# Two hybrid layers on one core: score products of the keys' low parts over all 128 rows, in key blocks of 512 and 256 columns

## The chip, the cores and the metric

The kernel runs on one core of a Trainium2 chip. The metric is the device time of one execution in microseconds (us). Before the change the median of three runs is 2503.3 us (2502.24 to 2503.67).

## The reference, cut to what matters

Two layers act on 512 latent tokens and 256 context tokens with 2048 features. A layer modulates its input, projects it, passes three groups of columns on (a short convolution, differential attention, pooling), gates them, projects back and normalizes. The change lies in the attention. There are 8 heads; each has two halves of 64 features, and for each half a score of a query block against all keys:

```python
s = jnp.einsum('bqhid,bkhid->bhiqk', qb * ATTN_SCALE, k_all)   # i: the two halves, d: 64 features
p = jax.nn.softmax(s, axis=-1)
a = p[:, :, 0] - lam * p[:, :, 1]
return jnp.einsum('bhqk,bkhe->bqhe', a, v_all)
```

Latent queries see 768 keys (context and latents). In the first layer the context's queries see the 256 context keys; in the second layer the context has no queries. All arrays are float32, and the kernel keeps nearly that precision.

## The kernel before, in words

**Precision by parts.** Each float32 operand x is split into a high part (a copy in the type F32R, made by ScalarE) and a low part (x minus the high part, made by VectorE). A product of two operands is then three matmuls, high x high, high x low, low x high, that add up in one PSUM bank (mm3, line 322).

**Weights.** WStream (line 144) loads pieces of 128x512 floats through SyncE's queue into six rotating buffers raw (RAW = 6, line 146). `_split` (line 164) copies one to wh on ScalarE, subtracts on VectorE into wl, and issues the load that follows; four pairs wh and wl rotate (BUFS = 4). Until late in the startup two raw loads stand ahead; from then on as many as there are buffers (line 440).

**Order.** The program is written out by hand. Every engine works through its own instructions in order; a matmul "slot" of the projections ends with pump() (line 220), which runs the due steps (later, line 217), one step of the attention of a head (att), and, if VectorE's estimated time leaves room, one step of the background queue (modq), which computes modulation vectors on VectorE from weights that are loaded by SyncE (mod_gen, line 462). The estimates are dve_cost and pe_cost (lines 65 and 72).

**Stages.** In each layer: four feature tiles and v (startup for layer 0, line 370; lines 1220 to 1241 for layer 1), the remaining feature tiles with the attention of the heads beside them (mtile, line 738, called in line 1259), then the output projection (gemm2, line 1066). TensorE's work of the feature tiles is interleaved with that of the attention.

**Head tiles.** alloc_head_tiles (line 520) makes for each layer the tiles Q (tag z2, 2048 columns), K (three rows of 768), aT and v (2048 columns). Q and v have unused tails of 512 columns, and the background work writes its unneeded elementwise results there (Z["jk"], lines 524 and 530). v_evac (line 535) uses the first 1024 columns of Q, v, K and aT for evacuating the rows of v.

**Queries and keys of a head.** For the halves i = 0 and 1, Q[:, i] has 128 rows: the 64 high parts and the 64 low parts of that half. The high parts stand in rows 0 to 63 for i = 0 and in rows 64 to 127 for i = 1. K[:, i] has the high parts of the keys of that half twice, in both groups of rows, so that one full-row product gives high x high and low x high. The low parts of the keys are in K[:, 2]: half 0 in rows 0 to 63, half 1 in rows 64 to 127 (ev_k, line 812; los, lines 825 and 826). So the product with the low parts uses 64 rows only (hi, line 599). rq is the work row of 768 columns in which queries and keys are turned.

**A score** (score, line 597) has a step mm, which issues the products (lines 615 to 618), and a step ex, which takes the maximum on VectorE (line 623) and the exponential on ScalarE (line 624), both from PSUM. For 768 keys, four products are issued: full-row for keys 0 to 383 and 384 to 767, in a bank each, then 64-row for the same; for the 256 context keys one of each. Two PSUM pairs SS are used in turn by the scores and the transposes of the result (trans, line 640); pvmm (line 666) then multiplies by v. A layer 0 head has 4 query blocks with 768 keys and 2 with 256, a layer 1 head 4 with 768, each for two halves.

Of the kernel before, what the change touches and what calls it, by code (L numbers as in the profile page):

```python
# [10 lines left out]
F32 = mybir.dt.float32  # L11
# [30 lines left out]
class Timed:  # L42
    """an engine, with an estimate of the time that its queue takes"""

# [33 lines left out]
def body(tc, A, out):  # L78
# [4 lines left out]
    with tc.tile_pool(name="sb", bufs=1) as sb, tc.tile_pool(  # L83
# [3 lines left out]
        def st(shape, name, dt=F32, tag=None, bufs=1):  # L87
            return sb.tile(shape, dt, name=name, tag=tag or name, bufs=bufs)

# [1 line left out]
        ident = st([P, P], "ident")  # L91
# [22 lines left out]
        edge = st([P, 4, 16], "edge")  # L114
        pw = st([P, P], "pw")
        neglam = st([P, 2], "neglam")
        sc1 = st([P, KT, 2], "sc1")
# [19 lines left out]

# [1 line left out]
        wseq = []  # L139
# [4 lines left out]
        class WStream:  # L144
            """weights: DRAM -> raw -> exact high and low parts"""
            BUFS, RAW = 4, 6

# [48 lines left out]

# [1 line left out]
        att = deque()  # L198
# [21 lines left out]
        def pump(n=1):  # L220
            for _ in range(n):
                slotn[0] += 1
                for fn in due.pop(slotn[0], ()):
                    fn()
                step(att)
                # the background takes what time VectorE has left
                V.t = max(V.t, PE.t - LAG)
                credit[0] = min(credit[0] + rate[0], 3.0)
                if modq and credit[0] >= 1 and V.t < PE.t - left[0]:
                    credit[0] -= 1  # L230
                    step(modq)
# [6 lines left out]

# [1 line left out]
        S.dma_start(out=bm, in_=A["bm"])  # L240
# [11 lines left out]
        def silu2_into(dst, tmp):  # L252
            """dst = 2 * silu(dst)"""
            S.activation(out=tmp, in_=dst, func=AF.Tanh, scale=0.5)
            V.scalar_tensor_tensor(out=dst, in0=tmp, scalar=1.0, in1=dst, op0=ALU.add, op1=ALU.mult)
# [14 lines left out]

        # consumption order of the projections' weights
        first4 = [M_CC, M_CU, M_CB, M_CG]
# [16 lines left out]
        lt = [layer_tiles(l) for l in range(2)]  # L289
        # pieces of the last weights that wait on chip: split beside these pairs  # L290
        SIDE = [(1, 3), (1, 6)] + [(2, j) for j in range(8)]
# [18 lines left out]

        # token accumulators of the token-major products
        accs = [lat[0], lat[1], SS[0][:, 0], SS[0][:, 1], SS[1][:, 0], SS[1][:, 1]]

        # what can be read after the products of a token, as a pair of banks is waited for as a whole
        ready = [[0], [1], [], [2, 3], [], [4, 5]]
# [16 lines left out]

# [1 line left out]
        # The scales come first: the feature tiles are of the scaled rows and get the shifts' part as a bias  # L334
        # later, the rows of v are of the whole h.
        NB = 4
# [33 lines left out]
        def startup():  # L370
# [11 lines left out]
            silu2_into(srows[0], pp.rearrange("p a b -> p (a b)")[:, 0:JD])  # L382
            # the other row to all partitions
            for j in range(0, JD, 512):
# [75 lines left out]

# [1 line left out]
        def mod_gen(tiles, nv, kcs, buf, rows=None):  # L462
            """acc: from the modulation's weights, or bv: the shifts' part of the first tiles"""
            sbm, rawm, jk = buf
# [35 lines left out]
        class Cvt:  # L500
            """rotating use of the three wide scratch rows"""

# [15 lines left out]
        Z = {}  # L518

        def alloc_head_tiles(l):  # L520
            q = st([P, 2048], f"Q_{l}", F32R, tag="z2")
            Z["Q"] = q[:, 0:2 * T].rearrange("p (a b) -> p a b", a=2)
            Z["Qf"] = q
            Z["jk"] = q[:, 2 * T:2 * T + KCH]
            Z["K"] = st([P, 3, T], f"K_{l}", F32R, tag="z0")
            Z["a"] = st([P, 2, 6, 256], f"aT_{l}", F32R, tag="z1")
            v = st([P, 2048], f"v_{l}", F32R, tag="z3")
            Z["v"] = v[:, 0:12 * P].rearrange("p (a b c) -> p a b c", a=2, b=6)
            Z["vf"] = v
            Z["jk"] = (Z["jk"], v[:, 12 * P:12 * P + KCH])  # L530

# [30 lines left out]

# [1 line left out]
        lb = [0]  # L564
# [19 lines left out]
        def attention(l, h):  # L584
# [12 lines left out]
            def score(t, qt, i):  # L597
                box = {}
                hi = slice(0, 64) if i == 0 else slice(64, 128)
                qs = slice(qt * P, qt * P + P)  # L600
# [4 lines left out]
                def mm():  # L605
                    s = box["t"] = next_S()
                    if qt < 4:
                        box["s"] = s[:, :, 0:384]
                        parts = [(s[:, 0, 0:384], 0), (s[:, 1, 0:384], 384)]
                        n = 384  # L610
                    else:
                        box["s"] = s[:, 0, 0:256]
                        parts = [(box["s"], 512)]
                        n = 256
                    for ap, k0 in parts:
                        PE.matmul(ap, lhsT=Q[:, i, qs], rhs=K[:, i, k0:k0 + n], start=True, stop=False)
                    for ap, k0 in parts:
                        PE.matmul(ap, lhsT=Q[hi, i, qs], rhs=K[hi, 2, k0:k0 + n], start=False, stop=True)
                    scores_left[0] -= 1

                def ex():
                    sv = box["s"]
                    V.tensor_reduce(out=sm[:, i:i + 1], in_=sv, axis=AX.XY if qt < 4 else AX.X, op=ALU.max, negate=True)
                    S.activation(out=po.rearrange("p (a b) -> p a b", a=2) if qt < 4 else po, in_=sv, func=AF.Exp,  # L624
                                 bias=sm[:, i:i + 1], scale=1.0, accum_out=sm[:, 2 + i:3 + i])
                    free_S(box["t"])
# [39 lines left out]
            def pvmm(t, u):  # L666
# [5 lines left out]
                def mm():  # L672
                    # beside the closed half of the features' bank that is not in use
                    pv = box["p"] = cps[(lb[0] + 1) % 2][:, 256:512]
                    for j, kt in enumerate(kts):
                        mm3(pv, v[:, 0, kt], v[:, 1, kt], a[:, 0, kt], a[:, 1, kt], j == 0, j == n - 1)
# [9 lines left out]
            scores_left[0] = 2 * nq  # L686
            # distances of the steps, in steps: two of them to a slot in layer 0, one in layer 1
            t, gs, gt, gp, dx, dn, dc, dl, dv, ge, gf = PAR[l]
# [46 lines left out]

# [1 line left out]

# [34 lines left out]
        def silu2(tmp, pl, pc, ctx):  # L772
            """tmp = 2 * silu(psum)"""
            for ps, a, b in segs(pl, pc, ctx):
# [4 lines left out]
        def rope():  # L779
# [7 lines left out]
            cvt.give(i)  # L787

        lo_, hi_ = slice(0, 64), slice(64, 128)

# [21 lines left out]
        def ev_k(l, h, pl, pc):  # L812
# [11 lines left out]
            def los():  # L824
                V.tensor_sub(out=K[lo_, 2], in0=rq[lo_], in1=K[lo_, 0].bitcast(F32))
                V.tensor_sub(out=K[hi_, 2], in0=rq[hi_], in1=K[hi_, 1].bitcast(F32))

# [148 lines left out]

# [1 line left out]
        yrow = lambda s: cv[:, s % 3, 0:T] if s % 6 < 3 else pp[:, s % 3, :]  # L978
# [14 lines left out]

# [1 line left out]
        def gate_row(t0, i, j):  # L995
# [8 lines left out]
        def h_affine():  # L1004
            for i in range(2):
                # h = n * (g (1 + sc)) + (b (1 + sc) + sh)
                V.tensor_scalar(out=hA[:, :, i], in0=acc[:, 32:48, i], scalar1=1.0, scalar2=None, op0=ALU.add)
# [58 lines left out]
        def gemm2(l):  # L1066
# [85 lines left out]
            flush()  # L1152
            # the last part token by token, so that the norms follow closely
            S.activation(out=rst[:, 0:1], in_=epsc, func=AF.Sqrt)
# [19 lines left out]
            else:  # L1174
# [5 lines left out]
                for t in range(4):  # L1180
# [4 lines left out]
                    S.activation(out=r, in_=mv[:, t, 1:2], func=AF.Sqrt, bias=epsc, scale=1.0)  # L1185
                    # a part of the first rows goes another way, so that VectorE keeps up with the products
                    own = hv[:1] if t < 2 else hv
# [16 lines left out]

# [1 line left out]
        for l in range(2):  # L1206
# [12 lines left out]
            else:  # L1219
                # four feature tiles of the latents, as their h arrives  # L1220
                for k in range(KT):
# [117 lines left out]
```

## Time and profile before

| what | value |
|---|---|
| median of three runs | 2503.3 us (2502.24 to 2503.67) |
| span of the profiled execution, first to last instruction | 2499.2 us |
| the profiled execution's own time | not listed apart; the median is 4.1 us over its span |
| TensorE (PE) busy | 2462.3 us, 99% |
| TensorE weight loads (PEld) busy | 2032.7 us, 81% |
| VectorE (DVE) busy | 1696.4 us, 68% |
| ScalarE (ACT) busy | 927.8 us, 37% |
| GpSimd (POOL) busy | 121.0 us, 5% |
| moved by DMA | 353.64 MB, 141 GB/s |
| mean granted TensorE clock, as a share of the full one | 0.995 |

The profile comes from one execution. Busy time is the union of an engine's instructions. Matmuls are pipelined and overlap, so a matmul's listed duration is longer than what it costs in a dense stream; the distance between the starts of neighbours is the cost. Every matmul has a weight load of its own, listed under PEld, which can run beside the matmul ahead of it. In square brackets a row tells how long the engine was idle before it, and which instruction's end released it.

### The profile page before, as it was taken

What the parts mean: (1) busy time and instruction counts of PE and PEld (TensorE: products, weight loads), DVE (VectorE), ACT (ScalarE), POOL (GpSimd) and SP (SyncE); (2) the same over time, 40 slices, a digit from 0 to 9 for tenths busy, and PEclk for the clock granted to TensorE, in tenths of its full rate; (3) what the DMA queues carried; (4) which work ended last, traced back from release to release, by engine and by line L of the source; (5) the groups of instructions that cost most, each with busy time, mean ns of one, the idle gap of its engine ahead of it and who ended that gap; (6) DMA issues with size and microseconds to landing.
All of it is one profiled execution on the core that took longest, in us unless ns stands there. A gap on an engine that the chain in (4) does not pass through costs nothing. (4 is left out here: it accounts for less than half of the span.)

```text
span 2499.2 us, 33724 instructions
## 1 busy us (share of the span) xinstructions
PE 2462.3 (99%) x12501; PEld 2032.7 (81%) x12501; DVE 1696.4 (68%) x3252; ACT 927.8 (37%) x1668; POOL 121.0 (5%) x197
## 2 busy tenths in 40 slices
PE   8999999999999999999999999999999999999997
PEld 7887888888888888888888778888878887887885
DVE  8894868677677778755486663256676666666656
ACT  4551434333343434433211253134444434444321
POOL 0000000000000000001100000000000000000202
PEclk9999999999999999999999999999999999999998
DMA  9886634343443434334455532253443434423653
GB/s 337 311 294 201 203 107 115 104 114 106 117 115 95 125 103 123 91 91 137 168 172 172 178 114 89 97 184 93 120 127 111 118 98 128 122 81 110 201 157 131
DMA packets 182168, 353.64 MB, mean 141 GB/s; under 512 B 19217, under 2 KB 43937, under 8 KB 181234
## 3 DMA queue, kind: packets, MB, share of 16 engines
q1 hardware_dynamic: 144946, 293.88, 37.0%
q0 software_dynamic: 36912, 57.55, 8.2%
q8 instruction: 98, 1.61, 0.3%
q14 instruction: 68, 0.56, 0.1%
q10 hardware_dynamic: 144, 0.05, 0.0%
HBM read 319.89 MB, written 31.51 MB: 141 GB/s over the span
## 5 line engine op out<-in xcount | busy, mean ns | idle before, releaser
L53 DVE TENSOR_TENSOR wl<-raw,wh 128x512 fp32r<-128x512 f32 x566 | 384.4, 689 | 384.9 <-ACT wh L173 383.5
L53 PE MATMUL lat<-hhl,wh 128*128 128x512 f32 x1472 | 603.7, 410 | 1.6 <-DVE Q L53 1.6
L173 ACT CAST wh<-raw 128x512 fp32r<-128x512 f32 x566 | 346.5, 618 | 663.4 <-PE SS L53 289.5
L53 PE MATMUL lat<-hll,wh 128*128 128x512 f32 x1472 | 583.5, 396 | 0.0
L53 PE MATMUL lat<-hhl,wl 128*128 128x512 f32 x1472 | 582.8, 396 | 0.0
L53 PEld LDWEIGHTS lat<-hhl,wh 128*128 128x128 f32 x1472 | 277.8, 189 | 71.8 <-issue 22.0
L53 PEld LDWEIGHTS lat<-hhl,wl 128*128 128x128 f32 x1472 | 277.8, 189 | 65.1
L53 PE MATMUL cps<-hc,wh 128*128 128x256 f32 x1664 | 318.9, 285 | 0.1
L53 PEld LDWEIGHTS lat<-hll,wh 128*128 128x128 f32 x1472 | 278.3, 189 | 43.2 <-DVE hll L53 0.3
L53 PEld LDWEIGHTS cps<-hc,wh 128*128 128x128 f32 x1664 | 275.2, 189 | 39.5 <-issue 8.5
L624 ACT ACTIVATE pp<-SS,smt 128x768 f32<-128x768 f32 (+1 forms) x160 | 130.7, 817 | 355.1 <-DVE smt L53 349.6
L53 PE MATMUL cps<-hc,wl 128*128 128x256 f32 x832 | 231.5, 278 | 0.0
L53 PE MATMUL SS<-wh,hc 128*128 128x512 f32 x512 | 171.1, 393 | 0.4 <-DVE aT L53 0.3
L53 PEld LDWEIGHTS cps<-hc,wl 128*128 128x128 f32 x832 | 156.4, 188 | 0.0
L53 PE MATMUL SS<-K,Q 128*128 128x384 f32 (+1 forms) x576 | 155.6, 361 | 0.7 <-DVE aT L53 0.7
L53 PE MATMUL lat<-wl,hhl 128*128 128x512 f32 x364 | 144.9, 398 | 6.8 <-DVE wl L53 6.8
L53 PE MATMUL lat<-wh,hhl 128*128 128x512 f32 x364 | 146.3, 402 | 0.5 <-DVE o L53 0.5
L53 DVE TENSOR_REDUCE smt<-SS 128x1 f32<-128x768 f32 (+1 forms) x160 | 135.4, 846 | 16.7 <-PE SS L53 16.7
L53 PE MATMUL lat<-wh,hll 128*128 128x512 f32 x364 | 143.1, 393 | 0.0
L53 PEld LDWEIGHTS SS<-K,Q 128*128 128x128 f32 (+1 forms) x576 | 94.9, 186 | 48.0 <-issue 35.0
L53 DVE CUSTOM_DVE_ANT_0 pp<-cv,acc 128x512 bf16<-128x512 f32 x112 | 80.0, 748 | 52.2 <-DMA cv<-in_wmbg_dram 37.8
L53 PEld LDWEIGHTS SS<-wh,hc 128*128 128x128 f32 x512 | 96.3, 188 | 22.9 <-DVE aT L53 1.2
(263 smaller groups left out, 3561.9 us busy)
## 6 DMA issues: line engine op xcount, KB each, us to landing
raw<-in_wa_dram SPq DMA_DIRECT2D x352, 256.0 KB, 2.7
m<-in_wmbg_dram SPq DMA_DIRECT2D x200, 256.0 KB, 2.7
raw<-in_wo_dram SPq DMA_DIRECT2D x128, 256.0 KB, 3.2
wb<-in_wm0b_dram SPq DMA_DIRECT2D x32, 704.0 KB, 7.1
raw<-in_wv_dram SPq DMA_DIRECT2D x64, 256.0 KB, 3.3
cv<-in_wmbg_dram SPq DMA_DIRECT2D x56, 256.0 KB, 2.7
cv<-in_xT_dram SPq DMA_DIRECT2D x32, 384.0 KB, 4.9
v<-vsc POOLq DMA_DIRECT2D x32, 384.0 KB, 6.0
```

The source lines that it names most:

```text
L53: return fn(*a, **k)
L173: S.copy(out=h, in_=r)
L624: S.activation(out=po.rearrange("p (a b) -> p a b", a=2) if qt < 4 else po, in_=sv, func=AF.Exp, bias=sm[:, i:i + 1], scale=1.0, accum_out ...
```

## The change

The keys' low parts get rows of zeros, so that they have 128 rows. For half 0 they remain in K[:, 2], whose rows 64 to 127 are now zero. For half 1 they move to the tail of Q (512 columns) and the last 256 columns of v, with zeros in rows 0 to 63. The zeros are written once per layer: GpSimd fills rq with zeros, and ScalarE copies from it. The low products use the whole of Q[:, i]; key blocks are now 512 and 256 columns, and the order is high, low for each block. The subtraction for half 1 becomes two. The unneeded results of the background work go to a tile jk of their own in bfloat16, and the raw buffers are five. Scores of 768 keys are read from PSUM as one flat row. Comment lines that the diff only empties are left out here.

```diff
@@ persistent tiles
+        jk = st([P, KCH], "jk", BF16)
@@ class WStream
-            BUFS, RAW = 4, 6
+            BUFS, RAW = 4, 5
@@ alloc_head_tiles
+        lo_, hi_ = slice(0, 64), slice(64, 128)
+
         def alloc_head_tiles(l):
             q = st([P, 2048], f"Q_{l}", F32R, tag="z2")
...
-            Z["jk"] = q[:, 2 * T:2 * T + KCH]
...
-            Z["jk"] = (Z["jk"], v[:, 12 * P:12 * P + KCH])
+            Z["jk"] = (jk, jk)
+            K = Z["K"]
+            Z["Kl"] = [(K[:, 2, 0:512], K[:, 2, 512:T]), (q[:, 2 * T:2 * T + 512], v[:, 14 * P:16 * P])]
+            G.memset(rq, 0.0)
+            for part, rows in zip(Z["Kl"], (hi_, lo_)):
+                for x, c in zip(part, (slice(0, 512), slice(512, T))):
+                    S.copy(out=x[rows], in_=rq[rows, c])
@@ score
-                hi = slice(0, 64) if i == 0 else slice(64, 128)
...
                 def mm():
                     s = box["t"] = next_S()
+                    lo = Z["Kl"][i]
                     if qt < 4:
-                        box["s"] = s[:, :, 0:384]
-                        parts = [(s[:, 0, 0:384], 0), (s[:, 1, 0:384], 384)]
-                        n = 384
+                        box["s"] = s.rearrange("p a b -> p (a b)")[:, 0:T]
+                        parts = [(s[:, 0], K[:, i, 0:512], lo[0]), (s[:, 1, 0:256], K[:, i, 512:T], lo[1])]
                     else:
                         box["s"] = s[:, 0, 0:256]
-                        parts = [(box["s"], 512)]
-                        n = 256
-                    for ap, k0 in parts:
-                        PE.matmul(ap, lhsT=Q[:, i, qs], rhs=K[:, i, k0:k0 + n], start=True, stop=False)
-                    for ap, k0 in parts:
-                        PE.matmul(ap, lhsT=Q[hi, i, qs], rhs=K[hi, 2, k0:k0 + n], start=False, stop=True)
+                        parts = [(box["s"], K[:, i, 512:T], lo[1])]
+                    for ap, kh, kl in parts:
+                        PE.matmul(ap, lhsT=Q[:, i, qs], rhs=kh, start=True, stop=False)
+                        PE.matmul(ap, lhsT=Q[:, i, qs], rhs=kl, start=False, stop=True)
                     scores_left[0] -= 1
 
                 def ex():
                     sv = box["s"]
-                    V.tensor_reduce(out=sm[:, i:i + 1], in_=sv, axis=AX.XY if qt < 4 else AX.X, op=ALU.max, negate=True)
-                    S.activation(out=po.rearrange("p (a b) -> p a b", a=2) if qt < 4 else po, in_=sv, func=AF.Exp,
+                    V.tensor_reduce(out=sm[:, i:i + 1], in_=sv, axis=AX.X, op=ALU.max, negate=True)
+                    S.activation(out=po, in_=sv, func=AF.Exp,
@@ ev_k, los
                 V.tensor_sub(out=K[lo_, 2], in0=rq[lo_], in1=K[lo_, 0].bitcast(F32))
-                V.tensor_sub(out=K[hi_, 2], in0=rq[hi_], in1=K[hi_, 1].bitcast(F32))
+                for x, c in zip(Z["Kl"][1], (slice(0, 512), slice(512, T))):
+                    V.tensor_sub(out=x[hi_], in0=rq[hi_, c], in1=K[hi_, 1, c].bitcast(F32))
```

## Rows read from the trace of the kernel before

**Rows 1.** The page: span, and TensorE's busy time, share and instructions.

```profile
span 2499.2 us, 33724 instructions
...
PE 2462.3 (99%) x12501; PEld 2032.7 (81%) x12501; DVE 1696.4 (68%) x3252; ACT 927.8 (37%) x1668; POOL 121.0 (5%) x197
```

**Rows 2.** Attention stretches: length, busy PE, PEld, DVE, ACT, POOL, PEclk, DMA share, GB/s.

```profile
260.00:1165.00 905.00, 902.23 (x5130) 759.36 (x5130) 662.64 (x1381) 344.48 (x650) 28.67 (x44) 1.00 0.40 114
...
1657.00:2305.00 648.00, 647.25 (x3139) 519.63 (x3138) 430.01 (x750) 281.81 (x491) 25.41 (x39) 1.00 0.38 112
```

**Rows 3.** TensorE's groups by shape: the score products (busy, mean ns, idle before).

```profile
L53 PE MATMUL SS<-K,Q 64*128 64x384 f32 x256 | 78.8, 387 | 0.0
L53 PE MATMUL SS<-K,Q 128*128 128x384 f32 x256 | 66.9, 342 | 0.7 <-DVE aT L53 0.7
...
L53 PE MATMUL SS<-K,Q 64*128 64x256 f32 x32 | 12.1, 380 | 0.0
```

**Rows 4.** Timeline of TensorE, a layer 1 score (start, duration); narrow windows split the four.

```profile
1990.79 1.06 PE L53 MATMUL SS<-K,Q 128*128 128x384 f32 x4
...
1990.96 0.34 PE L53 MATMUL SS<-K,Q 128*128 128x384 f32 x1
...
1991.23 0.44 PE L53 MATMUL SS<-K,Q 64*128 64x384 f32 x1
...
1991.51 0.34 PE L53 MATMUL SS<-K,Q 64*128 64x384 f32 x1
...
1991.78 0.50 PE L53 MATMUL lat<-hhl,wh 128*128 128x512 f32 x1
1992.11 0.39 PE L53 MATMUL lat<-hll,wh 128*128 128x512 f32 x1
1992.35 0.39 PE L53 MATMUL lat<-hhl,wl 128*128 128x512 f32 x1
```

**Rows 5.** Timeline of the weight loads beside the same score.

```profile
1991.23 0.29 PEld L53 LDWEIGHTS SS<-K,Q 64*128 64x128 f32 x2 [0.25 <-issue]
...
1992.12 0.19 PEld L53 LDWEIGHTS lat<-hhl,wl 128*128 128x128 f32 x1
```

**Rows 6.** Timeline of TensorE, a layer 0 score of 256 keys.

```profile
366.24 0.28 PE L53 MATMUL cps<-hc,wl 128*128 128x256 f32 x1
366.36 0.59 PE L53 MATMUL SS<-K,Q 128*128 128x256 f32 x2
...
367.45 0.39 PE L53 MATMUL lat<-hhl,wl 128*128 128x512 f32 x1
```

**Rows 7.** Instructions on tiles K and Q: ns min/median/max, first and last start, forms.

```profile
L53 DVE TENSOR_TENSOR K<-rq,K x32: 942/950/957, 297.3 to 2230.4; 64x768 fp32r<-64x768 f32 x32
...
L53 DVE TENSOR_TENSOR Q<-rq,Q x32: 684/820/957, 281.5 to 2206.2; 64x768 fp32r<-64x768 f32 x16, 64x512 fp32r<-64x512 f32 x16
...
L803 ACT CAST Q<-rq x16: 616/725/836, 279.2 to 2202.7; 64x768 fp32r<-64x768 f32 x8, 64x512 fp32r<-64x512 f32 x8
```

**Rows 8.** Timeline of ScalarE and of TensorE after the startup.

```profile
185.18 0.59 ACT L543 CAST K<-SS 128x512 fp32r<-128x512 f32 x1 [0.79 <-PE SS L53]
...
189.83 0.50 PE L53 MATMUL SS<-wh,hc 128*128 128x512 f32 x1 [0.34 <-DVE aT L53]
```

**Rows 9.** Raw weight loads: time to landing, and SyncE's timeline late in layer 1.

```profile
DMA to landing us min/median/max: 2.4/2.8/9.9
...
2388.74 34.58 SPq L159 DMA_DIRECT2D raw<-in_wo_dram  x21
```

**Rows 10.** The page's costliest groups: background work with results in bfloat16.

```profile
L53 DVE CUSTOM_DVE_ANT_0 pp<-cv,acc 128x512 bf16<-128x512 f32 x112 | 80.0, 748 | 52.2 <-DMA cv<-in_wmbg_dram 37.8
```

**Rows 11.** Tile Q: background work that writes its tail; waits of its instructions for PE.

```profile
L53 DVE CUSTOM_DVE_ANT_0 Q<-m,acc x136: 739/746/754, 345.3 to 2190.7; 128x512 fp32r<-128x512 f32 x136
...
  PE lat L53: 2.4, 3
```

**Rows 12.** TensorE's groups by shape: the products with v.

```profile
L53 PE MATMUL cps<-aT,v 128*128 128x256 f32 x624 | 82.5, 284 | 1.4 <-DVE aT L53 1.4
```

More of the change, by code (lines that the diff above doesn't have):

```diff
@@ L787, in rope @@
             cvt.give(i)
-        lo_, hi_ = slice(0, 64), slice(64, 128)
         def ev_q(l, h, pl, pc):
```

## The prediction, made before the result was known

> **What bounds the kernel now.** I read the page's busy table first: TensorE (PE) is busy for 2462.3 of 2499.2 us [rows 1]. Then the busy time by stage: the two stretches that hold the attention (260 to 1165 us for layer 0, 1657 to 2305 us for layer 1) have PE at 902.23 of 905 us and 647.25 of 648 us, at a granted clock of 1.00, the upper of its two levels (2.4 GHz), while VectorE (DVE) stands at 662.64 and 430.01 us, 73% and 66%, and ScalarE (ACT) below 44% [rows 2]. So a product that becomes shorter there should bring the end nearer by as much, unless something else is late next.
>
> A busy PE isn't PE at its best, so the next view is the groups by shape: the score products of 384 columns are 256 full-row ones (128 rows) and 256 of 64 rows, and there are 32 of 64 rows and 256 columns, each behind a full-row one [rows 3]. So 256 / 2 = 128 scores have 768 keys (four products) and 32 have 256 keys (two). The mean durations there overlap, so they price nothing; what counts is the distance from start to start, in the timeline.
>
> **The edit that should matter: full rows instead of 64.** In one score of layer 1 the starts are 1990.79, 1990.96, 1991.23, 1991.51, and the first product of the projection follows at 1991.78, the second at 1992.11, the third at 1992.35 [rows 4]. Undisturbed full-row products give the scale: the two full-row score products stand 0.17 us apart for 384 columns, and the projection's 512 columns take 0.24 us (1992.11 to 1992.35, rounded; 0.17 x 512 / 384 is 0.23, which I use). Against 0.17, the step from full rows to 64 costs 0.27 (0.10 too much), the first 64-row product 0.28 (0.11), the last one before full rows return 0.27 (0.10), and the first full-row product after it 0.33 instead of 0.23 (0.10). The last one counts, as its duration shows: it took 0.50 us where its neighbours took 0.39. The weight loads agree: the loads of the 64-row products begin at 1991.23, with their own product, after 0.25 us without a load, whereas an ordinary one begins at 1992.12, 0.01 us after the product before its own [rows 5]. So a change of row form stops the stream and leaves the next weight load uncovered, once on the way in and once on the way out.
>
> The sum per score goes by the whole stretch, not by the rounded parts: 1990.79 to 1992.35 is 1.56 us for four score products and two of the projection. After the change the four are 512, 512, 256 and 256 columns, all full-row. A full-row 256-column product takes 0.12 us (366.24 to 366.36 [rows 6]), so they take 0.23 + 0.23 + 0.12 + 0.12 = 0.70, with two projection products of 0.23 makes 1.16. Saved: **0.40 us** for a score of 768 keys. For one of 256 keys, 366.36 to 367.45 is 1.09 us for two score and two projection products; afterwards 2 x 0.12 + 2 x 0.23 = 0.70. Saved: **0.39 us**. The columns streamed are the same 768 + 768 before and after, and rows of zeros are streamed like others, so the new split by itself adds nothing. The order high, low, high, low into one bank is that of the projections, which run at the 0.23 and 0.12 above.
>
> Sum: 128 x 0.40 + 32 x 0.39 = 51.2 + 12.5 = **63.7 us**, 38.1 in layer 0 and 25.6 in layer 1.
>
> The Trainium skill, TensorEngine Tiling (Array Packing), section Key Properties, says that changing the tiling mode, unlike changing the tile, drains the engine. The trace agrees on the place: two disturbances per score, however many 64-row products lie between. Counted as bare drains (0.10 on the way in, 0.10 out) that rule gives 160 x 0.20 = 32 us and some 2476 us; the rows have the two late loads on top.
>
> **What it adds elsewhere.** The low parts of the second half of the heads: one DVE subtraction of 64x768 (0.95 us) becomes one of 64x512 (0.684, the shortest of the same form on Q) and one of 64x256 (estimate: 768 against 512 columns is 0.957 - 0.684 = 0.273, so 0.684 - 0.273 = 0.41) [rows 7]. That is +0.15 us x 16 heads = 2.3 us of DVE time, hidden by the 242 and 218 us in which DVE idles in the two stretches; uncovered it would be 2.3 us.
>
> The zeros: per layer one GpSimd fill of 128x768 and four ACT copies, 64x512 twice at about 0.62 [rows 7] and 64x256 twice, between 0.2 and 0.62; 1.6 to 2.5 us of ACT, I take 2.0. GpSimd issues no transfer that is waited for at that point, and in layer 0 the fill can run early in the startup, as its row buffer is free then; bounds 0 and one or two us, taken as 0. The copies stand ahead of the evacuations of v's first half on ACT. There ACT waits 0.79 us for PE before one evacuation, and PE in turn waits 0.34 us for an evacuated accumulator at 189.83 [rows 8]. The gap takes up 0.79 of the 2.0 us, and the evacuations behind it wait for PE's tokens too: bounds 0 and 2, taken 0.5 us. In layer 1 they fall beside projection work with weights already split ahead: 0, at most 2.
>
> Five raw weight buffers for six: a load is still issued behind each split, one buffer later in the sequence. Landing takes 2.8 us in the median and 9.9 at most [rows 9]. In the densest stretch, in the last products of layer 1, 21 loads are issued in 34.58 us, 1.65 us each; the four loads that remain ahead cover 4 x 1.65 = 6.6 us, five cover 8.2. At 2.8 us nothing is late: 0. If all of them took 9.9 us, 9.9 / 4 = 2.5 us each would add 0.85 x 21 = 18 us: the upper bound. I take 0, as the median is much nearer, and split weights wait ahead of PE besides. SyncE's queue waits no longer than before: the new load waits for the same split; the mod loads behind it likewise. The junk outputs in bfloat16 in a tile of their own replace a write of the same 512 elements; the bfloat16 form, on a scratch tile, takes 748 ns [rows 10], the other 746 [rows 11]: 0, and a few ns either way are in DVE's idle time. The reduction and the exponential read the same 768 elements from two banks as one flat row: 0; a tenth of a microsecond each way on 160 of them, hidden by ACT's and DVE's idle time, is the bound.
>
> **What is late next.** Between a score and its transposes lies a chain of DVE and ACT work; its places in the program are fixed, and PE reaches them up to 0.4 us sooner. Now PE waits 1.4 us in all before the 624 products of v with the attention's rows [rows 12]. Nothing lost is the lower bound; the upper is 1 us for each of 16 heads, 16 us, over ten times today's sum. I take 0.25 us per head, 4 us, since DVE keeps over a fifth of its time: after the change it is busy 665 of 867 us and 431 of 622, 77% and 69%.
>
> Net: 63.7 - 4 - 0.5 = 59 us. On the profiled execution's own scale the span goes from 2499.2 to 2440; the median of the runs is 2503.3, 4.1 us more than that span, and the same 59 us off it is **2444 us**.
>
> **Rivals.**
> A, DVE becomes the bound in attention. For it: it is the next busiest, and its work comes in bursts. Against: 27% idle. If waits of 1 us a head appear, 16 instead of 4 us are given back: 2456.
>
> B, the raw buffers run dry in layer 1's last products. For: the longest landing, 9.9 us, is over the 6.6 that four cover. Against: the median. Half the bound, 9 us: 2453.
>
> C, full-row score products don't hide their weight loads. Then each of 576 would pay the 0.11 us that the late loads show above, 63 us, and nothing is gained: 2503, no change. Against it: the load at 1992.12 [rows 5]. The Trainium skill, TensorE: Matmul & The Clock Gate, section The mechanism (Part 3), speaks for C and against this change: it has a weight load overlap running products only where its row group differs. The trace differs: the uncovered loads are those whose row group changes, and the covered one has the same rows as the product that it runs beside.
>
> D, slower: the second half's low parts now lie in the tails of the Q and v tiles. If waits went by tile, the subtraction in los (line 826) would stand on DVE until PE had done the previous head's products with v, and the splits of weights queued behind it would come late. It decides from (59 + 5) / 16 = 4 us of PE per head; at 4.2 us it is 67 us: 2511. Against: today 136 junk writes of DVE go to the tail of the Q tile, which PE reads all along, and the only wait for PE in that tile's list is 2.4 us for lat, an evacuation [rows 11]; waits go by region.
>
> **How the numbers follow.** Forecast 0.78, A 0.11, B 0.06, C 0.02, D 0.03. A measurement here tells about 0.2% from no change, 5 us. Forecast, A and B are faster: 0.95; C 0.02; D 0.03. The lower end is the full 63.7 us with no new wait and the rounding of the starts in 160 x 0.40 (0.01 us each is 1.6): 2503.3 - 63.7 - 1.6 is 2438, less one of margin for the median of runs: 2437. The upper end takes in A and B singly, with the two microseconds of the zero copies: 2458.
>
> **What would show it.** The profile after: no 64-row products, 576 full-row ones; score starts 0.23, 0.23, 0.12, 0.12 apart and the next projection product 0.39 long; the attention stretches some 37 and 24 us shorter, the others unchanged within 1 us; PE's waits for DVE in them a few us. It would be wrong if score products stay 0.1 us too far apart (C), if PE waits for smt, aT or wl over 10 us (A, D), or if weight splits wait for raw landings after layer 1's attention (B).

## The result, and the profile after

The kernel after takes 2441.84 us (median of four runs, 2439.96 to 2443.36), the one before 2502.82 us on the same chip: a ratio of 0.9758, 95% interval 0.9744 to 0.9772, 61 us less. The prediction was 2444 us, between 2437 and 2458. The span of the profiled execution goes from 2499.2 to 2440.6 us, 58.6 us less, where 2440 was forecast.

The page of the kernel after shows first that TensorE remains the bound, with as many matmuls as before [rows 1].

```profile
span 2440.6 us, 33840 instructions
...
PE 2398.7 (98%) x12501; PEld 2025.5 (83%) x12501; DVE 1697.2 (70%) x3268; ACT 927.0 (38%) x1676; POOL 123.2 (5%) x199
```

PE's busy time fell by 63.6 us; VectorE's (DVE) rose by 0.8. Next the score that stands for the one in [rows 4], in the timeline of TensorE (start, duration, instruction):

```profile
1944.02 0.39 PE L53 MATMUL SS<-K,Q 128*128 128x512 f32 x1
1944.24 0.40 PE L53 MATMUL SS<-Q 128*128 128x512 f32 x1
1944.48 0.28 PE L53 MATMUL SS<-K,Q 128*128 128x256 f32 x1
1944.59 0.28 PE L53 MATMUL SS<-v,Q 128*128 128x256 f32 x1
1944.71 0.39 PE L53 MATMUL lat<-hhl,wh 128*128 128x512 f32 x1
1944.94 0.39 PE L53 MATMUL lat<-hll,wh 128*128 128x512 f32 x1
1945.18 0.39 PE L53 MATMUL lat<-hhl,wl 128*128 128x512 f32 x1
```

From the first score product to the third projection product are 1.16 us, against 1.56 before: 0.40 less. The low products read Q's and v's tails here, hence their names. The first projection product after the score takes 0.39 us like any other, no longer 0.50. The weight loads beside it, which answer to [rows 5], each begin at or just after the start of the product ahead of their own (1944.02 under the product of 1944.02, 1944.60 under that of 1944.59), and the profile lists no idle time before any of them:

```profile
1944.02 0.19 PEld L53 LDWEIGHTS SS<-Q 128*128 128x128 f32 x1
1944.25 0.19 PEld L53 LDWEIGHTS SS<-K,Q 128*128 128x128 f32 x1
1944.48 0.19 PEld L53 LDWEIGHTS SS<-v,Q 128*128 128x128 f32 x1
1944.60 0.19 PEld L53 LDWEIGHTS lat<-hhl,wh 128*128 128x128 f32 x1
```

For a score of 256 keys, the timeline has what answers to [rows 6]; 366.55 to 367.24 is 0.69 us for two score and two projection products, against 1.09:

```profile
366.55 0.40 PE L53 MATMUL SS<-K,Q 128*128 128x256 f32 x2
...
367.24 0.40 PE L53 MATMUL lat<-hhl,wl 128*128 128x512 f32 x1
```

To see where the time went, both traces were cut at the same matmuls (TensorE's sequence has 12501 in both): the 1500th, just ahead of the first score, the 6300th, after layer 0's attention, the 8600th, ahead of layer 1's, and the 11700th, after it. The busy time of these stretches, first of the kernel before, then of the kernel after (length, busy PE, PEld, DVE, ACT, POOL; granted clock; DMA share, GB/s):

```profile
0.00:293.07 293.07, 283.66 (x1501) 241.11 (x1501) 233.15 (x440) 131.63 (x240) 9.93 (x22) 1.00 0.81 279
293.07:1139.94 846.87, 845.15 (x4802) 709.56 (x4801) 622.02 (x1296) 320.03 (x602) 21.63 (x32) 1.00 0.38 107
1139.94:1657.98 518.04, 509.51 (x2302) 417.78 (x2300) 285.55 (x585) 144.86 (x255) 32.55 (x60) 0.99 0.47 151
1657.98:2297.56 639.58, 639.04 (x3102) 513.16 (x3101) 426.84 (x745) 277.85 (x483) 23.64 (x36) 1.00 0.38 109
2297.56:2499.20 201.64, 184.93 (x803) 151.06 (x801) 128.89 (x187) 53.40 (x91) 33.27 (x48) 0.96 0.49 164
```

```profile
0.00:296.28 296.28, 284.51 (x1500) 241.22 (x1501) 234.67 (x440) 133.19 (x244) 10.69 (x23) 0.99 0.81 275
296.28:1108.41 812.13, 807.72 (x4801) 705.58 (x4801) 622.91 (x1304) 317.39 (x602) 21.94 (x32) 1.00 0.39 112
1108.41:1624.32 515.91, 507.34 (x2301) 415.12 (x2301) 285.20 (x585) 146.59 (x259) 33.39 (x61) 1.00 0.48 151
1624.32:2238.85 614.53, 614.14 (x3102) 512.77 (x3102) 425.94 (x753) 276.34 (x483) 23.68 (x36) 1.00 0.39 114
2238.85:2440.60 201.75, 185.04 (x803) 150.85 (x802) 128.52 (x187) 53.51 (x91) 33.48 (x48) 0.96 0.49 165
```

The attention of layer 0 is 34.7 us shorter, that of layer 1 25.0 us. The start is 3.2 us longer, the output projection of layer 0 with the start of layer 1 2.1 us shorter, the end the same. 34.7 + 25.0 + 2.1 - 3.2 is the 58.6 us. Length less busy time is what TensorE left unoccupied: from 1.7 to 4.4 us in the attention of layer 0, from 0.5 to 0.4 in that of layer 1. Its busy time fell by 37.4 and 24.9 us there, 62.3 for the 160 scores. In TensorE's groups by shape (busy, mean ns, idle time and releaser), these two have the new waits; they answer to [rows 12] and to the transposes, which did not wait before:

```profile
L53 PE MATMUL cps<-aT,v 128*128 128x256 f32 x624 | 82.4, 283 | 2.1 <-DVE aT L53 2.0
L53 PE MATMUL SS<-ident,pp 128*128 128x128 f32 x416 | 58.7, 273 | 1.8 <-ACT pp L631 1.8
```

### The profile page after: what moved, and what is told of

It is laid out like the page before. It is cut to its first block, busy times and chain, and to the rows that moved or that the text cites. A ratio compares the mean times of both kernels' runs of the same rounds, so it can differ in the third digit from the quotient of the medians.

```text
span 2440.6 us, 33840 instructions
## 1 busy us (share of the span) xinstructions
PE 2398.7 (98%) x12501; PEld 2025.5 (83%) x12501; DVE 1697.2 (70%) x3268; ACT 927.0 (38%) x1676; POOL 123.2 (5%) x199
## 5 line engine op out<-in xcount | busy, mean ns | idle before, releaser
L53 PE MATMUL lat<-hhl,wh 128*128 128x512 f32 x1472 | 590.9, 401 | 2.4 <-DVE Q L53 2.4
L53 PE MATMUL cps<-hc,wh 128*128 128x256 f32 x1664 | 313.3, 282 | 0.1
L53 DVE CUSTOM_DVE_ANT_0 jk<-m,acc 128x512 bf16<-128x512 f32 x224 | 166.9, 745 | 20.4 <-DMA m<-in_wmbg_dram 16.9
L53 PE MATMUL SS<-K,Q 128*128 128x256 f32 (+1 forms) x432 | 110.6, 334 | 0.7 <-DVE aT L53 0.7
```

The lines of the kernel that those rows point to most:

```text
L53: return fn(*a, **k)
```

## The experiments

**1. Only five raw buffers.** The kernel before, with one edit:

```diff
-            BUFS, RAW = 4, 6
+            BUFS, RAW = 4, 5
```

> The kernel before with five raw buffers and nothing else. Theory (the whole gain is in the row form of the score products): the loads stay ahead of the splits, 2503 us, within 2 us of the kernel before. Rival B of the prediction: weights come late in the last products of layer 1, up to 9 us more, 2512 us.

Measured: 2501.43 us against 2501.85, ratio 1.0003 (0.9992 to 1.0013). The stretches from the first score on, cut at the same matmuls:

```profile
293.60:1140.50 846.90, 845.19 (x4801) 708.74 (x4801) 621.74 (x1296) 320.08 (x602) 21.62 (x32) 1.00 0.38 107
1140.50:1661.30 520.80, 511.27 (x2302) 417.61 (x2301) 285.38 (x585) 144.89 (x256) 32.51 (x60) 0.99 0.47 150
1661.30:2300.90 639.60, 639.05 (x3103) 512.35 (x3102) 426.61 (x745) 278.06 (x483) 23.58 (x36) 1.00 0.38 109
2300.90:2502.85 201.95, 185.15 (x802) 150.72 (x801) 128.59 (x187) 53.64 (x91) 33.30 (x48) 0.96 0.50 165
```

846.9 and 639.6 us are those of before to within 0.1, and the last stretch, where rival B was placed, has 0.3 us more. The second row, around the change of layers, is 2.8 us longer: TensorE is unoccupied for 1.0 us more, with waits of 1.5 us in all for evacuations by VectorE that were not there before, and busy for 1.8 us more. The buffers need not be the cause, for experiment 2, with six, has the same stretch longer still, and three traces of one and the same kernel scatter by 6 us there (see the end of the next section). The sixth buffer had no measurable worth, and B falls. What the edit gives is room: a raw buffer takes 512 floats, 2 KB, per partition, and jk takes 1 KB.

**2. The same products in another order.** The kernel before, 64-row low products, key blocks of 384, but high and low in turn:

```diff
                     for ap, k0 in parts:
                         PE.matmul(ap, lhsT=Q[:, i, qs], rhs=K[:, i, k0:k0 + n], start=True, stop=False)
-                    for ap, k0 in parts:
                         PE.matmul(ap, lhsT=Q[hi, i, qs], rhs=K[hi, 2, k0:k0 + n], start=False, stop=True)
```

> The kernel before with 64-row low products, in the order high, low, high, low for the scores of 768 keys: same products, two more changes of row form in each of 128 scores. Theory (a change of row form costs 0.20 us each time, whatever the number of 64-row products between): 128 x 0.40 = 51 us more, 2554 us. Rival (a 64-row product is dearer by itself, by 0.2 us each or so): the same products in another order, no change, 2503 us.

Measured: 2550.78 us, ratio 1.0201 (1.0186 to 1.0217), 49 us more. The two attention stretches carry it, 871.94 and 664.50 us, 25.1 and 24.9 more than before:

```profile
293.69:1165.63 871.94, 870.24 (x4801) 715.81 (x4800) 622.97 (x1296) 320.64 (x602) 21.63 (x32) 1.00 0.36 104
1165.63:1687.61 521.98, 514.13 (x2301) 418.83 (x2300) 285.47 (x585) 144.98 (x255) 32.52 (x60) 0.99 0.47 150
1687.61:2352.11 664.50, 663.96 (x3102) 516.88 (x3101) 427.74 (x745) 279.13 (x483) 23.59 (x36) 1.00 0.36 105
```

64 scores of 768 keys in each layer at 0.39 us are 25.0. One of them in the timeline of TensorE; a first view merges the four score products, and narrow windows give the second, third and fourth apart:

```profile
2038.93 1.45 PE L53 MATMUL SS<-K,Q 128*128 128x384 f32 x4
...
2039.20 0.44 PE L53 MATMUL SS<-K,Q 64*128 64x384 f32 x1
...
2039.58 0.44 PE L53 MATMUL SS<-K,Q 128*128 128x384 f32 x1
...
2039.95 0.44 PE L53 MATMUL SS<-K,Q 64*128 64x384 f32 x1
...
2040.32 0.50 PE L53 MATMUL lat<-hhl,wh 128*128 128x512 f32 x1
2040.66 0.39 PE L53 MATMUL lat<-hll,wh 128*128 128x512 f32 x1
2040.89 0.39 PE L53 MATMUL lat<-hhl,wl 128*128 128x512 f32 x1
```

The weight loads beside it, in the timeline of PEld:

```profile
2039.20 0.18 PEld L53 LDWEIGHTS SS<-K,Q 64*128 64x128 f32 x1 [0.31 <-issue]
2039.58 0.19 PEld L53 LDWEIGHTS SS<-K,Q 128*128 128x128 f32 x1 [0.19 <-issue]
2039.95 0.18 PEld L53 LDWEIGHTS SS<-K,Q 64*128 64x128 f32 x1 [0.19 <-issue]
2040.32 0.19 PEld L53 LDWEIGHTS lat<-hhl,wh 128*128 128x128 f32 x1 [0.19 <-issue]
```

Behind every change the load begins only with its own product, the full-row one at 2039.58 too. A change of form ahead costs 0.27 - 0.17 = 0.10 us, and the product behind a change loses another 0.10: the products between two changes are 0.37 us apart, full-row and 64-row ones alike. The full-row product at 2039.58 takes 0.44 us here, where the one at 1990.96 took 0.34 [rows 4]. Whole score: 1.96 us for the stretch of 1.56. The order as such costs nothing: the kernel after also issues high and low in turn, with full rows, at 1.16 us. So it is the change that costs, 0.20 us each, not the 64-row product, and the rival falls.

**3. Full rows with the old key blocks.** The kernel after, with the low parts in blocks of 384 + 384 (the places for half 1 are both tails, 384 columns of each), both high products first, and the reads of PSUM by banks:

```diff
-            Z["Kl"] = [(K[:, 2, 0:512], K[:, 2, 512:T]), (q[:, 2 * T:2 * T + 512], v[:, 14 * P:16 * P])]
+            Z["Kl"] = [(K[:, 2, 0:384], K[:, 2, 384:T]), (q[:, 2 * T:2 * T + 384], v[:, 13 * P:16 * P])]
...
-                        box["s"] = s.rearrange("p a b -> p (a b)")[:, 0:T]
-                        parts = [(s[:, 0], K[:, i, 0:512], lo[0]), (s[:, 1, 0:256], K[:, i, 512:T], lo[1])]
+                        box["s"] = s[:, :, 0:384]
+                        parts = [(s[:, j, 0:384], K[:, i, 384 * j:384 * j + 384], lo[j]) for j in range(2)]
...
                     for ap, kh, kl in parts:
                         PE.matmul(ap, lhsT=Q[:, i, qs], rhs=kh, start=True, stop=False)
+                    for ap, kh, kl in parts:
                         PE.matmul(ap, lhsT=Q[:, i, qs], rhs=kl, start=False, stop=True)
```

> The kernel after, with all rows for the low products, but key blocks of 384 + 384 columns, both high products ahead of both low ones, and the two-bank reads of PSUM as before. Theory (the blocks don't matter, only the row form): 2442 us, within 2 us of the kernel after. Rival (the split into 512 + 256 and the flat reads have a share of the gain): between 2445 and 2503 us, in proportion to that share.

Measured: 2443.44 us, ratio to before 0.9767 (0.9750 to 0.9784), which holds the 0.9758 of the kernel after. Its attention stretches, 811.8 and 614.9 us, are within 0.4 us of those of the kernel after. The blocks of 512 and 256 and the flat reads have no measurable share.

**4. Half of the scores back on 64 rows.** The kernel after, with

```diff
+                    r = slice(0, 64) if i == 0 else slice(0, P)
                     for ap, kh, kl in parts:
                         PE.matmul(ap, lhsT=Q[:, i, qs], rhs=kh, start=True, stop=False)
-                        PE.matmul(ap, lhsT=Q[:, i, qs], rhs=kl, start=False, stop=True)
+                    for ap, kh, kl in parts:
+                        PE.matmul(ap, lhsT=Q[r, i, qs], rhs=kl[r], start=False, stop=True)
```

> The kernel after, with the low products of half 0 alone on 64 rows again (high, high, low, low), so 80 of 160 scores have a change of row form on the way in and one on the way out. Theory (0.40 us per such score, less what waits for VectorE took back): 80 x 0.40 = 32 us more than after, minus 1 to 2, 2472 us. Rival (the gain is a matter of the whole stage, such as fewer waits for other engines or the tiles' new places): no proportion to the number of scores, near 2442 or near 2503 us.

Measured: 2469.76 us, ratio to before 0.9875 (0.9860 to 0.9889), 28 us over the kernel after and 26 over experiment 3, which was timed beside it. The attention stretches are 827.77 and 626.69 us:

```profile
293.99:1121.76 827.77, 825.89 (x4801) 706.82 (x4800) 623.43 (x1304) 317.87 (x602) 21.63 (x32) 1.00 0.39 110
...
1640.07:2266.76 626.69, 626.29 (x3102) 512.97 (x3101) 426.51 (x753) 276.78 (x483) 23.91 (x36) 1.00 0.39 111
```

Against before that is 19.1 us for layer 0's 48 scores without changes of form and 12.9 us for layer 1's 32: 0.40 us each, nothing given back. The second half of the scores brought 15.6 and 12.2 us, 0.33 and 0.38 each. In layer 0, TensorE is unoccupied for 1.9 us here, against 1.7 before and 4.4 in the kernel after: with a stretch 2.3% shorter the new waits are not there, with one 4.1% shorter they are. The gain goes with the number of scores; only its last part meets other engines.

**5 to 10. The 3.2 us that the start lost.** Two edits were tried on the kernel after, each alone and both together, beside the kernel after itself (experiments 7 and 10). The copies of zeros were moved behind the first half of v, into the second:

```diff
             G.memset(rq, 0.0)
+        def zeros():
             for part, rows in zip(Z["Kl"], (hi_, lo_)):
...
-            v_phase(l, 1)
+            v_phase(l, 1, lambda j: zeros() if j == 3 else None)
```

and the junk of the background work went to two tiles in turn, as it had to two places before the change:

```diff
-            Z["jk"] = (jk, jk)
+            Z["jk"] = (jk, jk2)
```

> The kernel after, with the four copies of zeros of each layer moved from ahead of the evacuations of v's first half to the middle of v's second half. Theory (in layer 0 the copies stand ahead of the evacuations on ScalarE and cost TensorE 0.8 us at the first accumulator that is waited for and up to 0.5 us after it): TensorE's wait there goes from 1.3 back to 0.5 us, the start up to the attention becomes 1.0 to 1.3 us shorter, 2440.6 us. Rival (the start is longer for the shared junk tile, not for the copies): start as in the kernel after, 2441.8 us.

> The kernel of the run before with two junk tiles used in turn in place of one. Theory (VectorE starts a second junk product 0.12 us later when it writes the same tile as the one just ahead of it; before the change two places were used in turn): products that follow one another directly start 0.67 us apart in place of 0.79, the wait for the evacuation ahead of the first feature tile goes from 2.4 to about 1.6 us and the clock is likelier to stay up there, so the start becomes 0.8 to 2 us shorter than in the run before, 2439 us. Rival (the spacing has another cause): 0.79 us stays, no change.

> The kernel after, unchanged, on the same chip as the two runs ahead of it, for their comparison: 2441.8 us, within 2 us.

> The kernel after with two junk tiles in turn, the copies of zeros where the change has them. Theory (the two small losses are separate: about 1.5 us for the copies, 2 to 3 us for the shared junk tile): junk products 0.67 us apart, TensorE's wait at the first accumulator stays near 1.3 us over its stream, 2439 us. Rival (the gain of the run with both edits was one of chance in the clock and the loads): within 1 us of the kernel after.

> Copies of zeros late and two junk tiles, once more, beside the kernel after on the same chip: 4 to 5 us below it if the first comparison was no chance, within 1 us otherwise.

> The kernel after, unchanged, for the comparison with the two runs ahead of it: 2442 us, within 2 us.

| kernel | median us (range) | ratio to before (95%) |
|---|---|---|
| zeros late | 2440.09 (2438.80 to 2442.37) | 0.9765 (0.9745 to 0.9786) |
| both edits | 2436.60 (2435.10 to 2441.25) | 0.9753 (0.9732 to 0.9775) |
| after, beside these two | 2441.89 (2440.45 to 2443.83) | 0.9774 (0.9750 to 0.9798) |
| two junk tiles only | 2442.63 (2437.60 to 2444.16) | 0.9757 (0.9744 to 0.9770) |
| both edits again | 2441.18 (2439.89 to 2443.74) | 0.9756 (0.9743 to 0.9769) |
| after, beside these two | 2442.92 (2439.36 to 2446.87) | 0.9760 (0.9747 to 0.9773) |

In the times nothing is shown: the version with both edits was 5.3 us below the kernel after in one comparison and 1.7 in the other, where 4 to 5 had been expected again, with intervals that overlap. Two junk tiles alone came out 0.3 us below, as the rival had it. In the traces both mechanisms are plain. The wait of TensorE for an evacuated accumulator, which was 0.34 us before [rows 8], in the timeline of the kernel after and, in the second fence, of the kernel with the zeros late:

```profile
190.41 0.51 PE L53 MATMUL SS<-wh,hc 128*128 128x512 f32 x1 [1.18 <-DVE aT L53]
```

```profile
190.15 0.50 PE L53 MATMUL SS<-wh,hc 128*128 128x512 f32 x1 [0.32 <-DVE aT L53]
```

So the copies cost 0.86 us there, and moving them returns it: the wait is 1.1 or 1.2 us in the kernel after and experiments 7, 8 and 10, and 0.3 in experiments 5, 6 and 9, with the zeros late. The junk products, in the timeline of DVE, first with one tile (kernel after), then with two (both edits):

```profile
248.08 0.75 DVE L53 CUSTOM_DVE_ANT_0 jk<-m,mv 128x512 bf16<-128x512 f32 x1 [5.79 <-DMA m<-hrow]
248.75 0.08 DVE L53 DVE_READ_ACCUMULATOR2_ANT mv<- 128x1 f32 x1
248.87 0.75 DVE L53 CUSTOM_DVE_ANT_0 jk<-m,mv 128x512 bf16<-128x512 f32 x1
```

```profile
244.40 0.75 DVE L53 CUSTOM_DVE_ANT_0 jk<-m,mv 128x512 bf16<-128x512 f32 x1 [5.63 <-DMA m<-hrow]
245.07 0.08 DVE L53 DVE_READ_ACCUMULATOR2_ANT mv<- 128x1 f32 x1
245.07 0.75 DVE L53 CUSTOM_DVE_ANT_0 jk<-m,mv 128x512 bf16<-128x512 f32 x1
```

0.79 us from start to start with one tile, 0.67 with two. 47 products follow another that closely, 5.6 us of DVE in all, and none of it is seen at TensorE: the start, cut as above, takes 294.7 us in experiment 8 (two tiles) and 294.6 and 294.8 in experiments 7 and 10 (one tile). The wait ahead of the first feature tile, which experiment 6 was to shorten, is 2.4, 1.5 and 0.6 us in the three traces of the kernel after and so decides nothing.

## Why the prediction was right

**The saving per score** (0.40 and 0.39 us, sum 63.7) was right: 1.56 to 1.16 us and 1.09 to 0.69 in the timelines, and 25.0 us for layer 1's 64 scores where 25.6 were named. Over all scores it is 0.39 us, 62.3 of busy time for 160. That the loss belongs to the change of row form, once on the way in and once on the way out, was argued; experiment 2 shows it, with two more changes per score at 0.39 us, and 4 shows that it goes with the number of scores. The two parts of a change, 0.10 us in which the stream stops and 0.10 for the load behind it, were read from the starts; the loads of experiment 2 are late as described, but no run has one part without the other. The Trainium skill (TensorEngine Tiling (Array Packing), section Key Properties) says that a change of tiling mode drains the engine. Experiment 2 agrees with that; the price of a bare drain, as the prediction estimated it, would have been half of the gain, and the whole came.

**What is late next** (4 us) was right in size, in part by luck: of the 38.1 us forecast for layer 0 came 34.7, of the 25.6 for layer 1 25.0, 3.9 us less together. But only 2.5 of these are waits, 2.7 more in layer 0 and 0.2 less in layer 1; the other 1.4 are the 0.39 us per score. The place was only half named: the products with v wait 2.1 us instead of 1.4, but the transposes, where nothing was forecast, wait 1.8 us for the exponential on ScalarE. Rival A with 16 us falls.

**The zeros** (0 to 2 us, taken 0.5): 0.86 us at that wait, by experiment 5. In layer 1 no run shows a cost, but the stretch in question scatters by more than the 2 us of the bound.

**The five raw buffers** (0) and **the blocks and flat reads** (0) were right, by experiments 1 and 3. **The low parts of half 1** take 0.690 + 0.419 us per head, where 0.684 + 0.41 was estimated.

**The junk tile** (0) is the step that was wrong in kind, though not in what it cost: the durations of the two forms are the same, as read, but one tile for two products in a row sets them 0.12 us further apart.

**Rival C** falls with the loads above: each full-row score product's weights load under the product ahead. The Trainium skill (TensorE: Matmul & The Clock Gate, section The mechanism in Part 3) has a sentence by which a load overlaps running products only where its row group differs, and another that also lets a load for the background weight buffer go ahead. The loads above, in the same rows as the product that they run under, differ from the first.

**Rival D** falls: TensorE's and DVE's stretches show no waits of 4 us a head; layer 1's attention has 0.4 us of unoccupied PE.

**The other stretches** were to stay unchanged within 1 us, and did not: 3.2 us more at the start, 2.1 us less around the change of layers. That the two nearly cancel, so that the span came within 1 us of its forecast, is luck. In experiments 7 and 10, the same kernel at the full clock throughout the start, it is 1.7 and 1.5 us shorter, so about half of the 3.2 us is the clock (below); the zeros are 0.86, and the rest stays open. Around the change of layers these two traces have 518.0 and 521.8 us where the first trace of the same kernel has 515.9 and the kernel before 518.0, so the 2.1 us are within the scatter. The granted clock stood at the lower level there for 10.2 us in the profiled execution of before and for 3.4 us in that of after, but it does not explain the scatter alone: experiments 1 and 2 also have 10.2 us of it and take 2.8 and 3.9 us more than before.

## What to carry to other kernels

Look for matmuls whose contraction uses fewer rows than their neighbours': in a dense stream, each change between 64 and 128 rows cost 0.20 us here, about as much as streaming 440 columns (0.23 us for 512), and rows of zeros (free in stream time) remove it. Group what can't be padded, since two 64-row products in a row pay no more than one. Price such an edit by distances between starts over the whole stretch, up to the second product behind it, because half of the loss is in the duration of the neighbours, not in the suspicious instructions.

## What was not expected

A junk output can hold up VectorE: the start of a reduction that writes its unneeded result to the tile that the one just ahead of it writes came 0.12 us later (0.79 instead of 0.67 us), with no wait that the profile names.

The granted clock moved the comparisons by as much as the small edits. In the profiled execution of the kernel after, TensorE was idle for 2.38 us ahead of the first feature tile beside the attention, then ran more than 3.3 us at half clock (1.2 GHz):

```profile
257.89 0.54 PE L53 MATMUL lat<-hhl,wh 128*128 128x512 f32 x1 [2.38 <-DVE Q L53]
258.23 0.63 PE L53 MATMUL lat<-hll,wh 128*128 128x512 f32 x1
258.65 0.63 PE L53 MATMUL lat<-hhl,wl 128*128 128x512 f32 x1
```

The products are 0.42 us apart where they are 0.23 elsewhere; the busy times of this stretch (columns as above) show the granted clock at 0.50 behind POOL's:

```profile
258.30:261.60 3.30, 3.30 (x12) 2.82 (x11) 1.93 (x9) 2.90 (x6) 0.00 (x0) 0.50 1.02 343
```

The same kernel in experiment 7 stayed at the full clock there, after an idle time of 1.53 us. In experiment 8 an idle time of 2.32 us at the same place was followed by the full clock, so what makes the clock fall here stays open. The kernel after's spans in three profiled executions were 2440.6, 2438.7 and 2445.1 us, so a difference of 2 us is read from the trace or not at all.
